# Seven seven-product squares in three FFN-down sweeps and five in the last, with transposes for the second and third norm at a later place

## The chip, the core and the metric

The kernel runs on one core of one Trainium2 chip. Measured is the device time of one execution in microseconds (us); the median over several executions is compared. On the core, TensorE (PE; its weight loads are listed apart as PEld), VectorE (DVE), ScalarE (ACT) and GpSimd (POOL) work side by side, and SyncE (SP) issues the DMA transfers that bring weights from the chip's memory. The engines wait for each other by semaphores.

## What is computed

One layer of a decoder trunk over 256 tokens with 2048 channels, in float32: a mixer (causal pooling and an RWKV-7 scan), a squared-ReLU MLP with 8192 hidden channels, a gated embedding and a last norm. The part that matters here:

```python
def rms_norm(x, g):
    xf = x.astype(jnp.float32)
    y = xf * lax.rsqrt(jnp.mean(xf * xf, axis=-1, keepdims=True) + NORM_EPS)
    return (y * g.astype(jnp.float32)).astype(x.dtype)
...
        x = x + mix @ w_out[i]

        h2 = rms_norm(x, mlp_norm[i])
        x = x + jnp.square(jax.nn.relu(h2 @ w_ffn_up[i])) @ w_ffn_down[i]

        gate = jax.nn.sigmoid(rms_norm(x, ple_norm[i]) @ w_ple_gate[i])
        x = x + gate * (p[i] @ w_ple_proj[i])
    return rms_norm(x, final_norm)
```

## The kernel before

**Numbers in two parts.** Float32 operands are split into a high and a low part that PE multiplies at its fast rate. A weight tile `raw` is loaded by SP; ACT writes its high part `wh`, DVE the rest `wl = raw - wh`. A product is three matmuls of 128x512: high by high (L1228), high by low (L1229), low by high (L1230).

**The stages** follow each other: the mixer, w_out (tiles `o`), FFN-up and FFN-down (`u`, `d`), the embedding product (`pp`), the gate (`gt`) and the end. x is kept as two tiles, x0 and x1, of 128 tokens by 2048 channels. The FFN is done in two halves of 4096 hidden channels. A half computes eight blocks `u` into activations `y`, and then makes two *sweeps* of FFN-down, one for each 1024 output columns: d00 and d01 for the first half, d10 and d11 for the second. The name is d, half, column pair.

**Squares.** A sweep has 16 *squares*, kp = 0 to 15. A square multiplies a 2 by 2 block of activations with a 2 by 2 block of weights (two loads of 512 KB, rx and ry). A *normal* square takes the eight products, 24 matmuls, and two split weight tiles (`a` and `b`, from `halves_of`, each 128x1024 on DVE). A *seven-product* square (Strassen's form in Winograd's variant; kp in `SEVEN`) takes seven, 21 matmuls, but needs sums of weight blocks: four DVE operations of 128x512 into `td` (L1268 to L1271), one more split `wad` (L172, L173), and three split tiles of 128x1024 (`b`, `c`, `d`). It also needs sums of activations (tile S), which `activation_sums` forms once in each FFN half, while `u` runs, for both sweeps. `SEVEN` holds six squares; the last sweep uses four of them (1, 3, 6, 11).

**Banks.** The products gather in eight banks of PSUM: four single ones (`d_b`, the output blocks of normal products) and two double ones (`d_w`: w16 and w57). The double ones are also those of `u` and of the transposes `h2t` and `h3t`. After the last seven-product square DVE adds the double banks to x (L1248, L1288, L1292), and they come free; after the last square, the four closing adds bring the single banks to x.

**Transposes for norms.** `transposed` gives a `part(norm, n)`: eight PE transposes of 512 columns of x into a double bank, then for each 128 columns ACT and DVE write the high part and the rest (L1140, L1141; rows named `h`). For the second norm, part n follows w_out's column block n; part 3 needs w_out's last residual adds (L1071). For the third norm, parts 0 and 1 are called as `between` in the last sweep, at the end of square 11, parts 2 and 3 after the sweep.

**Gate weights ahead of time.** `keep`, called by hooks ahead of the squares in positions 5, 8, 11 and 14 of the last sweep and later four times more, loads a gate weight tile `graw` (L1170), and splits it on ACT (L1174) and DVE (L1175) into `gk`. The tag `graw` has two buffers; both are also taken by the high and the low part of the `d` tile of a seven-product square. So a `graw` load can start when a seven-product square has ended, and the next `d` tile waits until `gk` has been split.

**What sets the order.** From w_out on, a scheduler orders each engine's instructions from the order of the program and priorities: weight splits and the adds at the end of a sweep have a higher one and come earlier than they are written. In the sweeps d00, d01 and d10 PE runs in the order of the program; in d11 pieces of neighbouring squares and the `h3t` transposes are interleaved.

Of the kernel before, what the change touches and what calls it, by code (L numbers as in the profile page):

```python
# [10 lines left out]
F32R = mybir.dt.float32r  # L11
# [29 lines left out]
def trunk(  # L41
# [1053 lines left out]
    def wide_bank(name):  # L1095
        return psw.tile([128, 2, 512], F32, tag="wide", name=name)

    def gemm_wide(src, acts, name, consume):

        for half in range(2):
            bank = wide_bank(f"{name}_w{half}")
            for kq in range(4):
                raw = load_raw(src[half, kq].rearrange("p a n -> p (a n)"), 1024, f"{name}{half}_{kq}")
                for a, (wh, wl) in enumerate(split_w(raw, f"{name}{half}_{kq}")):
                    for b in range(2):
                        k = kq * 4 + 2 * a + b
                        hl = acts(k)
                        cs = [slice(b * 256 + ct * 128, b * 256 + ct * 128 + 128) for ct in range(2)]  # L1110
                        for ct in range(2):
                            nc.tensor.matmul(  # L1112
                                bank[:, ct, :].rearrange("p (s t) -> p s t", s=2), wh[:, cs[ct]], hl,
                                start=k == 0, stop=False, skip_group_check=True,
                            )
                        for ct in range(2):
                            nc.tensor.matmul(  # L1117
                                bank[:, ct, 0:T], wl[:, cs[ct]], hl[:, 0, :], start=False, stop=k == 15, skip_group_check=True
                            )
            consume(half, bank)  # L1120
# [27 lines left out]
    deep.append("w_out")  # L1148
    for n in range(4):
        run(gemm_toks(w_out[n], mix, f"o{n}", lambda banks: residual(banks, n), (6, 7, 2, 3)))  # L1150
        h2_part("mlp_norm", n)


    s2 = const.tile([128, 2], F32, name="s2sq")
# [30 lines left out]

    SEVEN = (1, 3, 6, 8, 11, 13)
    s_slots = (0, 2, 5)

    def activation_sums(box, kp, r):

        i = SEVEN.index(kp)
        if i % 2 == 0:
            box[kp] = box[SEVEN[min(i + 1, len(SEVEN) - 1)]] = a8(s_slots[i // 2], f"S{kp}", F32R)
        st = box[kp][:, i % 2 * 1024 : i % 2 * 1024 + 1024]
        t_ = fp.tile([128, 1024], F32, tag="junk", bufs=1, name=f"s{kp}")
        s1, s2_, s3, s4 = (t_[:, j * 128 : (j + 1) * 128] for j in range(4))
        a11, a21, a12, a22 = (r[:, j * 128 : (j + 1) * 128] for j in range(4))
        nc.vector.tensor_tensor(s1, a21, a22, op=ALU.add)  # L1200
        nc.vector.tensor_tensor(s3, a11, a21, op=ALU.subtract)
        nc.vector.tensor_tensor(s2_, s1, a11, op=ALU.subtract)
        nc.vector.tensor_tensor(s4, a12, s2_, op=ALU.subtract)
        split_sb(st[:, 0:512], st[:, 512:1024], t_[:, 0:512])

    def down_sweep(hf, pair, ys, sboxes, hooks=(), between=None, seven=SEVEN):
# [40 lines left out]
        def add(tt, c, src):  # L1247
            nc.vector.scalar_tensor_tensor(xs(tt, c), src, s2[:, tt : tt + 1], xs(tt, c), op0=ALU.mult, op1=ALU.add)  # L1248

        for q, kp in enumerate((0, 2, 1, 4, 3, *range(5, 16)) if pair else range(16)):  # L1250
            if q in hooks:
                hooks[q]()
            y, j = ys[kp // 2], kp % 2 * 512
            a11, a21, a12, a22 = ((y[:, j + i * 128 : j + i * 128 + 128], y[:, 1024 + j + i * 128 : 1152 + j + i * 128]) for i in range(4))
            rx, ry = (load_raw(w_down[pair, hf * 32 + 2 * kp + i], 1024, f"{nm}_{kp}_{i}") for i in range(2))
            if kp in seven:
                i = SEVEN.index(kp)
                st = sboxes[kp][:, i % 2 * 1024 : i % 2 * 1024 + 1024]
                s1, s2_, s3, s4 = ((st[:, c * 128 : c * 128 + 128], st[:, 512 + c * 128 : 640 + c * 128]) for c in range(4))
                t_ = a8(1, f"t{nm}_{kp}")  # L1260
                t1, t3, t2, t4 = (t_[:, c * 512 : c * 512 + 512] for c in range(4))
                wa = fp.tile([128, 1024], F32R, tag="wa", name=f"wa{nm}_{kp}")
                w11 = wa[:, 0:512], wa[:, 512:1024]
                with tc.high_priority(20000):
                    split_sb(*w11, rx[:, 0:512])
                w21, w22 = halves_of(ry, f"{nm}_{kp}b")
                with tc.high_priority(20000):
                    nc.vector.tensor_tensor(t1, rx[:, 512:1024], rx[:, 0:512], op=ALU.subtract)  # L1268
                    nc.vector.tensor_tensor(t3, ry[:, 512:1024], rx[:, 512:1024], op=ALU.subtract)
                    nc.vector.tensor_tensor(t2, t3, rx[:, 0:512], op=ALU.add)  # L1270
                    nc.vector.tensor_tensor(t4, ry[:, 0:512], t2, op=ALU.subtract)  # L1271
                w1, w3 = halves_of(t_[:, 0:1024], f"{nm}_{kp}c")
                w2, w4 = halves_of(t_[:, 1024:2048], f"{nm}_{kp}d", True)
                for n, a_, w_ in (("1", a11, w11), ("2", a12, w21), ("3", s4, w22), ("5", s1, w1), ("7", s3, w3), ("6", s2_, w2), ("4", a22, w4)):
                    prod(n, a_, w_)
            else:
                w11, w12 = halves_of(rx, f"{nm}_{kp}a")
                for n, a_, w_ in (("2", a11, w11), ("4", a21, w11), ("3", a11, w12), ("x", a21, w12)):
                    prod(n, a_, w_)
                w21, w22 = halves_of(ry, f"{nm}_{kp}b")  # L1280
                for n, a_, w_ in (("2", a12, w21), ("4", a22, w21), ("3", a12, w22), ("x", a22, w22)):
                    prod(n, a_, w_)
            if kp == seven[-1]:
                u = fp.tile([128, 512], F32, tag="r", bufs=2, name=f"u{nm}")
                with tc.high_priority(20000):
                    add(0, 0, b1)
                    nc.scalar.activation(u, b1, AF.Copy)
                    nc.vector.tensor_tensor(u, b6, u, op=ALU.add)  # L1288
                    add(0, 1, b5)
                    add(1, 1, b5)  # L1290
                    add(0, 1, u)
                    nc.vector.tensor_tensor(u, b7, u, op=ALU.add)  # L1292
                add(1, 0, u)
                add(1, 1, u)
                if between is not None:
                    between()
        for n, tt, c in (("2", 0, 0), ("4", 1, 0), ("3", 0, 1), ("x", 1, 1)):
            with tc.high_priority(30000):
                add(tt, c, banks[n])
# [1 line left out]
    def ffn_half(hf):  # L1301
        sboxes = {}
        ys = []
        for i in range(8):
# [10 lines left out]
                if 2 * i + bi in SEVEN:  # L1315
                    activation_sums(sboxes, 2 * i + bi, r)

            gemm_wide(w_up[f], h2, f"u{f}", square)
            ys.append(y)
            if f == 1:  # L1320
                inv_ms()
# [6 lines left out]
        if hf == 0:  # L1328
            down_sweep(hf, 1, ys, sboxes)
        else:  # L1330
            down_sweep(hf, 1, ys, sboxes, {5: keep, 8: keep, 11: keep, 14: keep}, lambda: [h3_part("ple_norm", n) for n in range(2)], (1, 3, 6, 11))
            for n in range(2, 4):
                h3_part("ple_norm", n)

# [149 lines left out]
```

## Time and profile before

| what | us |
|---|---|
| median of three runs | 1184.19 |
| lowest, highest | 1183.07, 1185.29 |
| the profiled run | 1184.84 |
| span in its profile | 1183.1 |
| PE busy | 1166.3 |
| DVE busy | 857.5 |
| ACT busy | 704.5 |

The profile shows one execution. A row of a timeline has start, duration, engine, line and operation, the tiles written and read, and, in brackets, how long the engine was idle before it and what released it. Durations of matmuls overlap: their pace is the distance from one start to the next. A row with xN stands for N like instructions that follow each other. The chain of waits is followed back from the last instruction; a row of it is the time that a piece adds to the end. A table by stretches gives, for each stretch, its length and then the busy time and count of PE, PEld, DVE, ACT and POOL, the granted clock of PE, the busy share of the DMA engines and GB/s.

### The profile page before, as it was taken

What the parts mean: (1) busy time and instruction counts of PE and PEld (TensorE: products, weight loads), DVE (VectorE), ACT (ScalarE), POOL (GpSimd) and SP (SyncE); (2) the same over time, 40 slices, a digit from 0 to 9 for tenths busy, and PEclk for the clock granted to TensorE, in tenths of its full rate; (3) what the DMA queues carried; (4) which work ended last, traced back from release to release, by engine and by line L of the source; (5) the groups of instructions that cost most, each with busy time, mean ns of one, the idle gap of its engine ahead of it and who ended that gap; (6) DMA issues with size and microseconds to landing.
All of it is one profiled execution on the core that took longest, in us unless ns stands there. A gap on an engine that the chain in (4) does not pass through costs nothing.

```text
span 1183.1 us, 17263 instructions
## 1 busy us (share of the span) xinstructions
PE 1166.3 (99%) x6428; PEld 976.6 (83%) x6428; DVE 857.5 (72%) x1156; ACT 704.5 (60%) x1302; POOL 13.6 (1%) x73
## 2 busy tenths in 40 slices
PE   9999999999999999999999999999999999999997
PEld 8787777888887888888888888888888888878886
DVE  7686995964656666667888977666678779788543
ACT  7776848676545465555565654554556555668544
POOL 2100000000000000000000000000000000000000
PEclk9999999999999999999999999999999999999999
DMA  8464443354455555656556665655555556767611
GB/s 290 151 198 148 130 144 122 119 179 157 163 199 177 178 181 194 193 184 209 196 183 209 210 217 178 193 185 193 188 188 205 203 195 207 275 219 252 197 54 71
DMA packets 60756, 216.81 MB, mean 183 GB/s; under 512 B 6784, under 2 KB 7552, under 8 KB 60288
## 3 DMA queue, kind: packets, MB, share of 16 engines
q1 hardware_dynamic: 60240, 215.12, 54.5%
q8 instruction: 50, 0.82, 0.3%
q10 hardware_dynamic: 432, 0.60, 0.1%
q14 instruction: 34, 0.28, 0.1%
HBM read 213.59 MB, written 2.10 MB: 182 GB/s over the span
## 4 chain that ended last, share of the span: by engine, by line
PE 95%; ACT 2%; DVE 1%; DMA 1%; issue 0%; POOL 0%; SPq 0%; ACTq 0%; POOLq 0%
PE u_w L1112 20%; PE u_w L1117 10%; PE d_b L1229 8%; PE d_b L1230 8%; PE d_b L1228 8%; PE gt_b L238 2%; PE gt_b L242 2%; PE gt_b L241 2%; PE d_w L1229 2%; PE d_w L1230 2%; PE d_w L1228 2%; PE zk_b L241 1%; PE zk_b L242 1%; PE o_b L241 1%; PE o_b L242 1%; PE zv_b L238 1%
## 5 line engine op out<-in xcount | busy, mean ns | idle before, releaser
L1112 PE MATMUL u_w<-h,wh_u 128*128 128x512 f32 x1024 | 322.2, 396 | 0.0
L167 ACT ACTIVATE wh_u<-raw_u 128x512 fp32r<-128x512 f32 x256 | 147.6, 624 | 163.1 <-issue 96.1
L168 DVE TENSOR_TENSOR wl_u<-raw_u,wh_u 128x1024 fp32r<-128x1024 f32 x128 | 156.7, 1225 | 110.9 <-ACT wh_u L167 109.0
L1117 PEld LDWEIGHTS u_w<-h,wl_u 128*128 128x128 f32 x1024 | 192.5, 188 | 45.1
L1117 PE MATMUL u_w<-h,wl_u 128*128 128x256 f32 x1024 | 201.5, 278 | 0.0
L1112 PEld LDWEIGHTS u_w<-h,wh_u 128*128 128x128 f32 x1024 | 156.0, 189 | 0.1
L168 DVE TENSOR_TENSOR wl_gt<-raw_gt,wh_gt 128x1024 fp32r<-128x1024 f32 x24 | 29.4, 1224 | 23.2 <-ACT wh_gt L167 23.1
L167 ACT ACTIVATE wh_gt<-raw_gt 128x512 fp32r<-128x512 f32 x48 | 28.0, 639 | 23.1 <-PE gt_b L242 14.4
L241 PE MATMUL gt_b<-wh_gt,h 128*128 128x512 f32 x96 | 37.4, 389 | 0.0
L242 PE MATMUL gt_b<-wh_gt,h 128*128 128x512 f32 x96 | 37.4, 389 | 0.0
L168 DVE TENSOR_TENSOR wl_o<-raw_o,wh_o 128x1024 fp32r<-128x1024 f32 x16 | 19.6, 1223 | 12.9 <-ACT wh_o L167 9.9
L167 ACT ACTIVATE wh_o<-raw_o 128x512 fp32r<-128x512 f32 x32 | 18.4, 623 | 16.2 <-issue 8.4
L167 ACT ACTIVATE wh_zp<-raw_zp 128x512 fp32r<-128x512 f32 x32 | 18.6, 623 | 15.9 <-PE zp_b L242 5.7
L168 DVE TENSOR_TENSOR wl_zk<-raw_zk,wh_zk 128x1024 fp32r<-128x1024 f32 x16 | 19.5, 1222 | 9.4 <-ACT wh_zk L167 9.3
L241 PE MATMUL zv_b<-wh_zv,hTh 128*128 128x512 f32 x64 | 26.0, 407 | 0.0
L241 PE MATMUL zk_b<-wh_zk,hTh 128*128 128x512 f32 x64 | 25.8, 404 | 0.0
L241 PE MATMUL zp_b<-wh_zp,hTh 128*128 128x512 f32 x64 | 25.7, 402 | 0.0
L238 PE MATMUL gt_b<-wl_gt,h 128*128 128x512 f32 x96 | 25.7, 389 | 0.0
L242 PE MATMUL zk_b<-wh_zk,hTl 128*128 128x512 f32 x64 | 25.6, 401 | 0.0
L241 PE MATMUL zr_b<-wh_zr,hTh 128*128 128x512 f32 x64 | 25.5, 398 | 0.0
L168 DVE TENSOR_TENSOR wl_zv<-raw_zv,wh_zv 128x1024 fp32r<-128x1024 f32 x16 | 19.4, 1219 | 8.2 <-ACT wh_zv L167 7.3
L242 PE MATMUL zp_b<-wh_zp,hTl 128*128 128x512 f32 x64 | 25.0, 391 | 0.0
(809 smaller groups left out, 2941.4 us busy)
## 6 DMA issues: line engine op xcount, KB each, us to landing
raw_u<-in_w_ffn_up_dram SPq DMA_DIRECT2D x128, 512.0 KB, 3.5
raw_d<-in_w_ffn_down_dram SPq DMA_DIRECT2D x128, 512.0 KB, 4.3
raw_gt<-in_w_ple_gate_dram SPq DMA_DIRECT2D x24, 512.0 KB, 3.4
raw_zk<-in_w_in_dram SPq DMA_DIRECT2D x16, 512.0 KB, 3.6
raw_zr<-in_w_in_dram SPq DMA_DIRECT2D x16, 512.0 KB, 3.4
raw_zv<-in_w_in_dram SPq DMA_DIRECT2D x16, 512.0 KB, 3.4
raw_zp<-in_w_in_dram SPq DMA_DIRECT2D x16, 512.0 KB, 3.3
raw_o<-in_w_out_dram SPq DMA_DIRECT2D x16, 512.0 KB, 4.1
```

The lines of the kernel that those rows point to most:

```text
L167: nc.scalar.activation(wh[:, a * 512 : (a + 1) * 512], raw[:, a * 512 : (a + 1) * 512], AF.Copy)
L168: nc.vector.tensor_tensor(wl, raw, wh.bitcast(F32), op=ALU.subtract)
L238: nc.tensor.matmul(banks[tt], ah[:, ts_], halves[a][1], start=False, stop=last)
L241: nc.tensor.matmul(banks[tt], ah[:, ts_], halves[a][0], start=i + a == 0, stop=False)
L242: nc.tensor.matmul(banks[tt], al[:, ts_], halves[a][0], start=False, stop=False)
L1112: nc.tensor.matmul(bank[:, ct, :].rearrange("p (s t) -> p s t", s=2), wh[:, cs[ct]], hl, start=k == 0, stop=False, skip_group_check=True,)
L1117: nc.tensor.matmul(bank[:, ct, 0:T], wl[:, cs[ct]], hl[:, 0, :], start=False, stop=k == 15, skip_group_check=True)
L1228: nc.tensor.matmul(banks[n], ah, wh, start=first, stop=False)
L1229: nc.tensor.matmul(banks[n], ah, wl, start=False, stop=False)
L1230: nc.tensor.matmul(banks[n], al, wh, start=False, stop=last)
```

## The change

`SEVEN` gets a seventh square, and its squares are now all odd ones up to 13: in d00, d01 and d10 seven squares take seven products, in d11 five (1, 3, 7, 9, 11). The seventh set of activation sums lies in a tile of its own. Sweep d01 takes its squares in another order, so that normal and seven-product ones alternate; d00 and d10 alternate in their natural order; d11 keeps its order. Part 3 of the second norm's transposes is no longer called after w_out's last block but inside `u0`, ahead of the second of its four quarters. Parts 0 and 1 of the third norm's are called after square 12 instead of at the end of square 11.

```diff
-    def gemm_wide(src, acts, name, consume):
+    def gemm_wide(src, acts, name, consume, amid=None):
...
             for kq in range(4):
+                if amid and half == 0 and kq == 1:
+                    amid()
...
-        h2_part("mlp_norm", n)
+        if n < 3:
+            h2_part("mlp_norm", n)
...
-    SEVEN = (1, 3, 6, 8, 11, 13)
+    SEVEN = (1, 3, 5, 7, 9, 11, 13)
...
-            box[kp] = box[SEVEN[min(i + 1, len(SEVEN) - 1)]] = a8(s_slots[i // 2], f"S{kp}", F32R)
+            st = a8(s_slots[i // 2], f"S{kp}", F32R) if i < 6 else fp.tile([128, 1024], F32R, tag="S", name=f"S{kp}")
+            box[kp] = box[SEVEN[min(i + 1, len(SEVEN) - 1)]] = st
...
-        for q, kp in enumerate((0, 2, 1, 4, 3, *range(5, 16)) if pair else range(16)):
+        for q, kp in enumerate(((0, 2, 1, 4, 3, *range(5, 16)) if hf else (0, 2, 1, 4, 3, 6, 5, 8, 7, 10, 9, 12, 11, 14, 13, 15)) if pair else range(16)):
...
-                if between is not None:
-                    between()
+            if kp == seven[-1] + 1 and between is not None:
+                between()
...
-            gemm_wide(w_up[f], h2, f"u{f}", square)
+            gemm_wide(w_up[f], h2, f"u{f}", square, None if f else lambda: h2_part("mlp_norm", 3))
...
-            down_sweep(hf, 1, ys, sboxes, {5: keep, 8: keep, 11: keep, 14: keep}, lambda: [h3_part("ple_norm", n) for n in range(2)], (1, 3, 6, 11))
+            down_sweep(hf, 1, ys, sboxes, {5: keep, 8: keep, 11: keep, 14: keep}, lambda: [h3_part("ple_norm", n) for n in range(2)], (1, 3, 7, 9, 11))
```

In the code of the change the lines lie some further down: L1232 to L1234 are the three matmuls of a product, L1244 the DVE part of a split tile, L1252 an add to x, L1272 to L1275 the four `td`, L1173, L1177 and L1178 the rows of `keep`, L1136 the transposes, L1114 and L1119 the matmuls of `u`, L1143 the DVE part of `h`. The rows below show order alone.

PE at the end of w_out and the start of u0, before:

```order
L238 MATMUL o3_b1_3652<-wl_o3_3_3713,mp1_3213 128x512
L1134 MATMUL h2t_3731<-ident_85,x0_2724 128x128
L1112 MATMUL u0_w0_3750<-h2_3359,wh_u00_0_3753 128x512 x2
L1117 MATMUL u0_w0_3750<-h2_3359,wl_u00_0_3754 128x256
L1134 MATMUL h2t_3731<-ident_85,x1_2725 128x128
L1134 MATMUL h2t_3731<-ident_85,x0_2724 128x128
L1134 MATMUL h2t_3731<-ident_85,x1_2725 128x128
```

The same place with the change:

```order
L238 MATMUL o3_b1_3652<-wl_o3_3_3713,mp1_3213 128x512
L1114 MATMUL u0_w0_3733<-h2_3359,wh_u00_0_3736 128x512 x2
L1119 MATMUL u0_w0_3733<-h2_3359,wl_u00_0_3737 128x256 x2
...
L1136 MATMUL h2t_3757<-ident_85,x0_2724 128x128
L1136 MATMUL h2t_3757<-ident_85,x1_2725 128x128
L1136 MATMUL h2t_3757<-ident_85,x0_2724 128x128
L1136 MATMUL h2t_3757<-ident_85,x1_2725 128x128
L1114 MATMUL u0_w0_3733<-h2_3359,wh_u00_1_3776 128x512 x2
```

Before, the first transpose of the last part stands right behind w_out's last matmul; now the whole first quarter of u0 (the first two u0 rows, four times over) is ahead of it.

DVE in the last sweep, on the way to the sums of square 11, before (the number behind d11_ is the square, the letter its split tile; `td` and `wad` are the weight sums of a seven-product square, `gk` a kept gate tile):

```order
L1240 TENSOR_TENSOR wl_d11_9a_9496<-raw_d11_9_0_9491,wh_d11_9a_9495 128x1024
L1175 TENSOR_TENSOR gk2_9569<-graw2_9567,gk2_9569 128x1024
L1240 TENSOR_TENSOR wl_d11_9b_9513<-raw_d11_9_1_9493,wh_d11_9b_9512 128x1024
L1268 TENSOR_TENSOR td11_11_9577<-raw_d11_11_0_9573 128x512
L173 TENSOR_TENSOR wad11_11_9578<-raw_d11_11_0_9573,wad11_11_9578 128x512
L1269 TENSOR_TENSOR td11_11_9577<-raw_d11_11_1_9575,raw_d11_11_0_9573 128x512
...
L1240 TENSOR_TENSOR wl_d11_10b_9551<-raw_d11_10_1_9531,wh_d11_10b_9550 128x1024
L1240 TENSOR_TENSOR wl_d11_11d_9596<-td11_11_9577,wh_d11_11d_9595 128x1024
L1240 TENSOR_TENSOR wl_d11_11b_9582<-raw_d11_11_1_9575,wh_d11_11b_9581 128x1024
L1240 TENSOR_TENSOR wl_d11_11c_9591<-td11_11_9577,wh_d11_11c_9590 128x1024
```

With the change:

```order
L1244 TENSOR_TENSOR wl_d11_9c_9555<-td11_9_9541,wh_d11_9c_9554 128x1024
L1178 TENSOR_TENSOR gk1_9495<-graw1_9493,gk1_9495 128x1024
L1244 TENSOR_TENSOR wl_d11_9d_9560<-td11_9_9541,wh_d11_9d_9559 128x1024
L1244 TENSOR_TENSOR wl_d11_10a_9590<-raw_d11_10_0_9585,wh_d11_10a_9589 128x1024
...
L173 TENSOR_TENSOR wad11_11_9634<-raw_d11_11_0_9629,wad11_11_9634 128x512
L1244 TENSOR_TENSOR wl_d11_11b_9638<-raw_d11_11_1_9631,wh_d11_11b_9637 128x1024
...
L1244 TENSOR_TENSOR wl_d11_11c_9647<-td11_11_9633,wh_d11_11c_9646 128x1024
L1178 TENSOR_TENSOR gk2_9625<-graw2_9623,gk2_9625 128x1024
L1244 TENSOR_TENSOR wl_d11_12a_9692<-raw_d11_12_0_9687,wh_d11_12a_9691 128x1024
L1244 TENSOR_TENSOR wl_d11_11d_9652<-td11_11_9633,wh_d11_11d_9651 128x1024
```

Square 9 is a seven-product one now, gk1 stands ahead of its `d` tile, and gk2 ahead of that of square 11; before, gk2 came two squares earlier, and square 9 had no sums.

SP in the last sweep, before and with the change:

```order
L158 DMA raw_d11_8_0_9453<-in_w_ffn_down_dram 128x1024
L1170 DMA graw0_9317<-in_w_ple_gate_dram 128x1024
L158 DMA raw_d11_8_1_9455<-in_w_ffn_down_dram 128x1024
L158 DMA raw_d11_9_0_9491<-in_w_ffn_down_dram 128x1024
L158 DMA raw_d11_9_1_9493<-in_w_ffn_down_dram 128x1024
L1352 DMA fn_9961<-in_final_norm_dram 128x2048
```

```order
L158 DMA raw_d11_8_0_9499<-in_w_ffn_down_dram 128x1024
L1356 DMA fn_10017<-in_final_norm_dram 128x2048
L1173 DMA graw0_9363<-in_w_ple_gate_dram 128x1024
L158 DMA raw_d11_8_1_9501<-in_w_ffn_down_dram 128x1024
L158 DMA raw_d11_9_0_9537<-in_w_ffn_down_dram 128x1024
L158 DMA raw_d11_9_1_9539<-in_w_ffn_down_dram 128x1024
```

The load of the final norm's weights (`fn`, 1 MB) stands ahead of the first gate tile's now, not behind it.

## The prediction

> **What bounds the kernel now.** I read the page first, then the chain of waits, then the busy time by stretches of the four FFN-down sweeps.
>
> ```profile
> span 1183.1 us, 17263 instructions
> PE 1166.3 (99%) x6428; PEld 976.6 (83%) x6428; DVE 857.5 (72%) x1156; ACT 704.5 (60%) x1302; POOL 13.6 (1%) x73
> PE 95%; ACT 2%; DVE 1%; DMA 1%; issue 0%; POOL 0%; SPq 0%; ACTq 0%; POOLq 0%
> ...
> 650.25 0.91 PE d_b L1228 x4
> ...
> 638.00:723.00 85.00, 85.00 (x376) 70.33 (x375) 72.93 (x82) 48.37 (x84) 0.00 (x0) 1.00 0.61 203
> 981.00:1074.00 93.00, 91.99 (x414) 75.63 (x414) 78.03 (x90) 58.23 (x106) 0.00 (x0) 1.00 0.72 247
> ```
>
> PE is busy 99% of the span and makes 95% of the chain. In the stretches (span of the stretch, then PE, PEld, DVE, ACT) sweep d01 (638 to 723) has PE busy for all of its 85 us, with DVE at 72.9: matmuls set the time, and a matmul less is time less as long as DVE keeps up. The last sweep, d11 (981 to 1074), has 1 us of PE idle and DVE at 78 of 93: least room. The clock column is 1.00 in both. The chain gives the price of a 128x512 matmul: 0.91 / 4 = 0.2268 us (the 0.39 of a single row overlaps its neighbour).
>
> **The change, term by term.** The profiled run took 1184.84 us with a span of 1183.1; 1.74 lies around the span, and the run is 0.65 above the median of 1184.19. I sum on the span and carry the difference to the median.
>
> *Fewer matmuls.* One more seven-product square in each of four sweeps: 3 matmuls less each, 4 x 3 x 0.2268 = **-2.72 us**.
>
> *The wait at the second norm.* The chain at the end of w_out:
>
> ```profile
> 378.12 0.69 PE o_b L238 x3
> 378.81 0.02 issue
> 378.83 0.70 DVE x L1071
> 379.54 0.04 issue
> 379.58 0.33 PE h2t L1134
> ```
>
> PE stands from 378.81 to 379.58, 0.77 us, since the transposes of the last columns need the last residual add. Now the first quarter of u0 (8 matmuls of 0.23, 8 of 0.12: 2.8 us) stands ahead of them, against two adds of 0.70: covered. The transposed part is needed only by the last quarter of u0; it is ready about 0.8 us ahead. **-0.77**; without the cover 0.
>
> *The wait at the third norm.* The first four rows of h3:
>
> ```profile
> 1058.83 0.39 PE L1228 MATMUL d_b<-wh_d_13b,y 128*128 128x512 f32 x1
> 1060.22 0.98 PE L1134 MATMUL h3t<-ident,x 128*128 128x128 f32 x7 [1.01 <-DVE h L1141]
> ...
> 1058.55 1.23 DVE L1240 TENSOR_TENSOR wl_d_14a<-raw_d,wh_d_14a 128x1024 fp32r<-128x1024 f32 x1 [1.33 <-ACT wh_d_14a L1239]
> 1059.69 0.87 DVE L1141 SCALAR_TENSOR_TENSOR h<-h3t,par_sb,h 128x256 fp32r<-128x256 f32 x2
> ```
>
> The last matmul's pace ends at 1058.83 + 0.23 = 1059.06; the second transposes start at 1060.22, after DVE has read the bank behind wl_14a: 1.16 us. They now stand behind half of square 14: **-1.16** for the old wait; what the new place costs comes below. All gains: 2.72 + 0.77 + 1.16 = 4.65.
>
> *Three sweeps with alternating squares.* A seven square needs three halves (wl), four td, one wad on DVE, a normal one two halves. Sweep d01 already alternates in the middle, squares 5 to 8:
>
> ```profile
> 671.99 1.23 DVE L1240 TENSOR_TENSOR wl_d_6c<-td,wh_d_6c 128x1024 fp32r<-128x1024 f32 x1 [1.17 <-ACT wh_d_6c L1239]
> 675.53 0.39 PE L1229 MATMUL d_w<-wl_d_6c,S 128*128 128x512 f32 x1
> 682.19 1.23 DVE L1240 TENSOR_TENSOR wl_d_8c<-td,wh_d_8c 128x1024 fp32r<-128x1024 f32 x1 [1.09 <-ACT wh_d_8c L1239]
> 685.73 0.39 PE L1229 MATMUL d_w<-wl_d_8c,S 128*128 128x512 f32 x1
> ```
>
> From the end of wl_6c (673.22) to its use is 2.31 us, of wl_8c (683.42) again 2.31: over one alternating pair the lead doesn't shrink. By the paces below a pair costs DVE 5 x 1.13 + 5 x 0.61 = 8.7 us against 45 matmuls, 10.2. So 0 here. If the lead shrank all the same, the extra squares of these sweeps would give back their 9 x 0.2268 = 2.04.
>
> *Two more sets of activation sums*, one in each half:
>
> ```profile
> L173 DVE TENSOR_TENSOR S<-s,S 128x512 fp32r<-128x512 f32 x12 | 8.2, 684 | 0.0
> L1200 DVE TENSOR_TENSOR s<-r 128x128 f32<-128x128 f32 x12 | 3.5, 293 | 0.4
> L168 DVE TENSOR_TENSOR wl_u<-raw_u,wh_u 128x1024 fp32r<-128x1024 f32 x128 | 156.7, 1225 | 110.9 <-ACT wh_u L167 109.0
> ```
>
> A set is four 128x128 at 0.29 and one split at 0.68: 1.84 us of DVE, 3.7 for both. In FFN-up DVE stands idle 110.9 us ahead of its wl rows, which covers them: 0, and 3.7 if that cover were gone.
>
> *The last sweep.* Here the gate weights kept for the end (gk) share two buffers with the d halves of seven squares, so a load starts when a seven square ends and must be split before the next one's d half:
>
> ```profile
> 1011.87 0.39 PE L1230 MATMUL d_b<-wh_d_3d,y 128*128 128x512 f32 x1
> 1012.06 0.33 SPq L1170 DMA_DIRECT2D graw<-in_w_ple_gate_dram  x1
> 1017.46 1.15 ACT L1174 ACTIVATE gk<-graw 128x512 fp32r<-128x512 f32 x2 [1.23 <-DMA graw<-in_w_ple_gate_dram]
> 1018.64 1.23 DVE L1175 TENSOR_TENSOR gk<-graw,gk 128x1024 fp32r<-128x1024 f32 x1 [1.16 <-ACT gk L1174]
> 1019.90 1.23 DVE L1240 TENSOR_TENSOR wl_d_6d<-td,wh_d_6d 128x1024 fp32r<-128x1024 f32 x1
> 1021.18 0.51 PE L1229 MATMUL d_w<-wl_d_6d,S 128*128 128x512 f32 x1
> ...
> DMA to landing us min/median/max: 4.3/5.4/7.4
> ...
> fn<-in_final_norm_dram SPq DMA_DIRECT2D x1, 1024.0 KB, 9.1
> ```
>
> From issue (1012.06) to the end of wl_6d (1021.13) are 9.07 us; from the end of square 3 (1012.10) PE has 40 matmuls, 9.07, up to its use. It has no margin today, and the next pairs get the same or less. The paces of DVE and its adds:
>
> ```profile
> 1009.46 1.22 DVE L1240 TENSOR_TENSOR wl_d_5a<-raw_d,wh_d_5a 128x1024 fp32r<-128x1024 f32 x1
> 1010.59 0.68 DVE L173 TENSOR_TENSOR wad<-raw_d,wad 128x512 fp32r<-128x512 f32 x1
> 1011.20 1.22 DVE L1240 TENSOR_TENSOR wl_d_5b<-raw_d,wh_d_5b 128x1024 fp32r<-128x1024 f32 x1
> ...
> 1016.26 1.23 DVE L1240 TENSOR_TENSOR wl_d_6c<-td,wh_d_6c 128x1024 fp32r<-128x1024 f32 x1 [2.11 <-ACT wh_d_6c L1239]
> ...
> 1048.82 1.40 DVE L1248 SCALAR_TENSOR_TENSOR x<-d_w,s2sq,x 128x512 f32<-128x512 f32 x2
> ```
>
> That is 1.13 us for a 128x1024, 0.61 for a 128x512, 0.66 for an add; two h rows take 0.87 by the row above. Then, place by place:
>
> - Square 7. In DVE's new order wl_7c stands behind gk0. Its use is 58 matmuls (13.15 us) after the end of square 3; behind the landing come gk's 1.15 on ACT, two 1.2 on DVE and their handovers, 4.7, so the load must land within 8.45. A 5.4 does; but fn, 1 MB, now stands ahead of graw0 on SP, and a landing of 9.1 would cost 0.65. I take 0.
> - Square 9. Load 1 goes out at the end of square 7, 40 matmuls before wl_9d is used: the chain above again. 0 at 5.4, 2.0 at 7.4, a gain below nothing is excluded since PE can't be early. I take 0.
> - Square 11. From wl_9d to wl_11d DVE now has seven 1.13 and five 0.61, 11.05 with a handover, ahead of PE's 48 matmuls, 10.89; gk2 and ACT's rows between may add waits like those in brackets (2.11, 1.16). By load: 7.4 + 4.8 = 12.2 against 43 matmuls, 9.75, so up to 2.4. I take 1.2, half.
> - The h3 transposes in square 14. From wl_11d, DVE has seven 1.13 (12b to 15a with gk3 and gk4), three 0.61, six 0.66 and three h: 7.91 + 1.83 + 3.96 + 1.3 = 15.0, and 1.2 for a half of ACT at its end, 16.2. PE has 68 matmuls and 8 transposes, 15.42 + 0.9 = 16.3. 0 if all flows, 2.4 with the same lateness of a load again. I take 1.2.
> - The end. gk6 moves ahead of DVE's four closing adds: 0 if its load is in, 0.7 for what its 1.13 takes of them, 2 with a late load. I take 0.
>
> Sum of new stalls **+2.4** (0 to 8.8).
>
> On load 0 the Trainium skill ("DMA: Bandwidth & Descriptors", section "Queues, rings and completion order") says that each DMA engine serves one queue's ring in order, so that a transfer on the same queue as a large one lies behind it. By that rule graw0 would land as late as fn and the forecast would be 0.65 higher, 1182.5; in before, fn stood behind the gate load, and no row shows the reverse.
>
> Sum: 1183.1 - 4.65 + 2.4 = 1180.85 span, 1182.6 as a profiled run, and 1184.19 - 2.25 = **1181.9** as a median.
>
> **The rivals.**
>
> *Clean last sweep.* Loads land by their median, DVE runs without gaps: stalls of 0 to 1.2, 1179.5 to 1180.7, say 1180.1. For it speaks that each chain just fits; against it the gaps of 1 to 2 us in the DVE rows of this very place.
>
> *Slower: the gate loads are late.* The mechanism is the pair of shared buffers: a load can't start before a seven square ends, and with 7, 9, 11 in alternation there is one normal square, 40 matmuls, between. If each of them takes the 7.4 that one load took, the stalls are 2.0 + 2.4 + 2.4, and 2.0 at the end with gk6 ahead of the adds: 6.8 to 8.8, or 1186.3 to 1188.3. It decides from 4.65 of stalls (slower at all), 7.0 (slower beyond 0.2%). For it: this stretch moves 247 GB/s against 203 in d01. Against it: the median of the eight is 5.4, and a PE that stalls gives the next load its time.
>
> *The change doesn't do what it says.* The three earlier sweeps don't gain: DVE can't hold seven alternating pairs, and the 2.04 go into short waits at every seven square; with the last sweep as forecast 1181.9 + 2.0 = 1184.0. Against it stands the constant lead of 2.31.
>
> **How the numbers follow.** Forecast (stalls 1.2 to 4, 1180.7 to 1183.5): 0.53. Clean: 0.20. Late loads: 0.17. No gain in three sweeps: 0.10. The time is the forecast's, 1181.9. The range leaves out the lowest part of the clean case and most of the late one: 1179.6 to 1185.6; the forecast's own is 1180.7 to 1183.5. 0.2%, about what a measurement tells from no change, is 2.37 us: faster is below 1181.8, slower above 1186.6. Half of the forecast (0.26) and the clean case (0.20) make faster 0.46; the late loads beyond 7.0 (0.14) and some of the rest slower 0.15; same 0.39.
>
> **What would show it.** Right: PE's matmul count 12 lower; no wait between w_out and u0; no waits of PE in d00, d01, d10; in d11 waits of about 1 us ahead of wl_11d and of the transposes in square 14. The clean case shows none there; the late one shows graw landings above 7 and waits of 2 us at each d half, and at gk6 before the closing adds. The prediction is wrong if PE waits in the first three sweeps, or if the last one loses more than 4 us, or if u0's last quarter waits for the moved transposes.

## The result and the profile after

The changed kernel takes 1181.92 us (median of 21 runs, 1180.22 to 1183.86), the kernel before 1183.69 (21 runs, 1181.89 to 1185.65): a ratio of 0.9986, with a 95% interval of 0.9980 to 0.9992. The predicted time was 1181.9. The median of before that the prediction started from, 1184.19, came from three runs; from the larger set the gain is 1.77 us, not the 2.25 that was forecast.

The page of the changed kernel, first rows (span; busy time, share and count of each engine):

```profile
span 1181.2 us, 17297 instructions
PE 1163.6 (99%) x6416; PEld 973.0 (82%) x6416; DVE 876.1 (74%) x1190; ACT 713.2 (60%) x1316; POOL 13.6 (1%) x73
```

PE has 12 instructions less (6428 before), DVE 34 more. PE still sets the end: it makes 94% of the chain of waits. To see where the 1.9 us of span went, I cut the PE timeline at fixed matmuls, and read the same marks in each kernel. In the changed kernel (start, duration, engine, line, operation):

```profile
377.03 1.07 PE L238 MATMUL o_b<-wl_o,mp 128*128 128x512 f32 x4
...
557.33 0.40 PE L1232 MATMUL d_b<-wh_d_0a,y 128*128 128x512 f32 x1
...
721.99 0.61 PE L1114 MATMUL u_w<-h,wh_u 128*128 128x512 f32 x2
...
900.33 0.40 PE L1232 MATMUL d_b<-wh_d_0a,y 128*128 128x512 f32 x1
...
1069.83 0.39 PE L1234 MATMUL d_b<-wh_d_15b,y 128*128 128x512 f32 x1
...
1084.69 0.39 PE L241 MATMUL gt_b<-wh_gt,h 128*128 128x512 f32 x1
```

and in the kernel before:

```profile
377.95 1.07 PE L238 MATMUL o_b<-wl_o,mp 128*128 128x512 f32 x4
...
558.88 0.40 PE L1228 MATMUL d_b<-wh_d_0a,y 128*128 128x512 f32 x1
...
724.95 0.62 PE L1112 MATMUL u_w<-h,wh_u 128*128 128x512 f32 x2
...
903.28 0.40 PE L1228 MATMUL d_b<-wh_d_0a,y 128*128 128x512 f32 x1
...
1073.65 0.39 PE L1230 MATMUL d_b<-wh_d_15b,y 128*128 128x512 f32 x1
...
1086.61 0.39 PE L241 MATMUL gt_b<-wh_gt,h 128*128 128x512 f32 x1
```

The first mark is the end of w_out (the start of its last row plus four matmuls at 0.2268). Then follow the first matmul of d00, the first of the second FFN-up, the first of d10, the last of d11 and the first of the gate product. The table gives the distances, in us, for the two kernels and for every experiment below. "d00 and d01" goes from the first d00 matmul to the second FFN-up, "d10 and d11" from the first d10 matmul to the start of the last d11 matmul. "sum" is the whole stretch from the end of w_out to the start of the last matmul; it includes the second FFN-up (178.33 or 178.34 in all) and the gate product (87.55 to 87.60). The ratio is to runs of before on the same chip.

| kernel | w_out to d00 | d00 and d01 | d10 and d11 | d11 to gate | sum | median us | ratio to before, 95% |
|---|---|---|---|---|---|---|---|
| before | 180.02 | 166.07 | 170.37 | 12.96 | 795.30 | 1183.69 | |
| change | 179.39 | 164.66 | 169.50 | 14.86 | 794.30 | 1181.92 | 0.9986 (0.9980 to 0.9992) |
| change, again (fifth) | 179.37 | 164.60 | 169.54 | 14.27 | 793.67 | 1182.84 | 0.9990 (0.9981 to 0.9998) |
| 1 gk6 behind the adds | 179.39 | 165.01 | 169.24 | 13.00 | 792.52 | 1182.42 | 0.9986 (0.9977 to 0.9994) |
| 2 third norm as before | 179.39 | 164.62 | 168.66 | 12.95 | 791.50 | 1181.21 | 0.9980 (0.9970 to 0.9990) |
| 3 second norm as before | 180.04 | 164.62 | 170.02 | 14.24 | 794.81 | 1184.42 | 1.0002 (0.9994 to 1.0011) |
| 4 fewer gk in the sweep | 179.39 | 164.64 | 169.82 | 12.97 | 792.71 | 1183.05 | 0.9990 (0.9982 to 0.9999) |
| 6 as 4, third norm as before | 179.39 | 164.64 | 169.95 | 12.96 | 792.82 | 1182.30 | 0.9993 (0.9982 to 1.0003) |
| 7 six squares in d11 | 179.40 | 164.67 | 168.98 | 13.51 | 792.50 | 1182.56 | 0.9990 (0.9981 to 0.9999) |
| 8 d01 in old order | 179.39 | 164.65 | 170.85 | 13.95 | 794.73 | 1182.52 | 0.9992 (0.9983 to 1.0001) |
| 9 gk behind the sweep | 179.37 | 164.64 | 168.39 | 13.18 | 791.47 | 1179.89 | 0.9969 (0.9957 to 0.9981) |
| 10 as 9, six squares | 179.37 | 164.63 | 167.64 | 13.24 | 790.79 | 1179.17 | 0.9964 (0.9950 to 0.9978) |
| 11 moves alone | 179.39 | 165.97 | 169.75 | 13.92 | 794.92 | 1185.08 | 1.0009 (1.0000 to 1.0018) |
| 12 before, gk behind | 180.05 | 166.04 | 169.10 | 12.95 | 794.03 | 1183.57 | 0.9994 (0.9985 to 1.0003) |

Two things are read off it. The columns repeat within a few hundredths where PE never waits. (The 165.01 of the first experiment holds a stop of 0.36 at the start of d01, where DVE's closing add that frees the bank came late, after waits of ACT and DVE for the load of a down weight; no other profile has it.) The part ahead of w_out's end, in which these kernels are alike, does not: it ended between 377.19 and 379.93 us in these profiles, 378.86 in before and 377.94 in the change. So 0.92 of the 1.9 us between the two spans is no work of the change; from w_out on this profile has gained 1.00, its repetition 1.63.

Where the loss sits, in the last sweep of the changed kernel, PE and then DVE:

```profile
1044.00 0.39 PE L1232 MATMUL d_b<-wh_d_12a,y 128*128 128x512 f32 x1
1044.40 0.50 PE L1233 MATMUL d_b<-wl_d_12a,y 128*128 128x512 f32 x1
1045.53 0.50 PE L1233 MATMUL d_w<-wl_d_11d,S 128*128 128x512 f32 x1 [0.63 <-DVE wl_d_11d L1244]
```

```profile
1040.42 1.23 DVE L1244 TENSOR_TENSOR wl_d_11c<-td,wh_d_11c 128x1024 fp32r<-128x1024 f32 x1 [0.50 <-ACT wh_d_11c L1243]
1041.98 1.23 DVE L1178 TENSOR_TENSOR gk<-graw,gk 128x1024 fp32r<-128x1024 f32 x1 [0.34 <-ACT gk L1177]
1043.12 1.22 DVE L1244 TENSOR_TENSOR wl_d_12a<-raw_d,wh_d_12a 128x1024 fp32r<-128x1024 f32 x1
1044.26 1.22 DVE L1244 TENSOR_TENSOR wl_d_11d<-td,wh_d_11d 128x1024 fp32r<-128x1024 f32 x1
```

Matmuls that should start 0.23 apart start 0.40 and 1.13 apart: 0.17 + 0.90, since wl_11d is fourth in DVE's line behind gk2 and wl_12a. No load is late here, as ACT's row of gk2 has no wait in front:

```profile
1040.81 1.14 ACT L1177 ACTIVATE gk<-graw 128x512 fp32r<-128x512 f32 x2
```

And at the end of d11, PE, then ACT and DVE:

```profile
1069.83 0.39 PE L1234 MATMUL d_b<-wh_d_15b,y 128*128 128x512 f32 x1
1071.74 0.33 PE L1136 MATMUL h3t<-ident,x 128*128 128x128 f32 x1 [1.53 <-DVE x L1252]
...
1149.97 0.39 PE L1388 MATMUL gt3a<-gk,h 128*128 128x512 f32 x1
```

```profile
1066.56 0.63 ACT L1177 ACTIVATE gk<-graw 128x512 fp32r<-128x512 f32 x1 [1.91 <-DMA graw<-in_w_ple_gate_dram]
1067.10 1.14 ACT L167 ACTIVATE wh_pp<-raw_pp 128x512 fp32r<-128x512 f32 x2
```

```profile
1068.27 1.23 DVE L168 TENSOR_TENSOR wl_pp<-raw_pp,wh_pp 128x1024 fp32r<-128x1024 f32 x1 [2.20 <-ACT wh_pp L167]
1069.42 0.48 DVE L1143 SCALAR_TENSOR_TENSOR h<-h3t,par_sb,h 128x256 fp32r<-128x256 f32 x1
1069.81 1.22 DVE L1178 TENSOR_TENSOR gk<-graw,gk 128x1024 fp32r<-128x1024 f32 x1
1070.94 2.72 DVE L1252 SCALAR_TENSOR_TENSOR x<-d_b,s2sq,x 128x512 f32<-128x512 f32 x4
```

PE's pace ends at 1070.06 and the next transpose starts at 1071.74: 1.68 us. Read backwards, the rows name the chain: the transpose waits for x, whose adds stand on DVE behind gk6, h and wl_pp; wl_pp waited 2.20 for ACT; ACT stood 1.91 at gk6's high part, whose load had not landed. One late load of a kept tile, none of which PE uses before 1149.97, 83 us later, holds two engines. The load was late because it could not start before DVE had split gk4 and freed the buffer (DVE, then SP):

```profile
1059.48 1.22 DVE L1178 TENSOR_TENSOR gk<-graw,gk 128x1024 fp32r<-128x1024 f32 x1
```

```profile
1060.73 0.33 SPq L1173 DMA_DIRECT2D graw<-in_w_ple_gate_dram  x1
```

It landed 5.8 us after its issue, and ACT was ready for it at 1064.65, 3.9 us after the issue. Of the eight kept tiles only one landed faster than that (3.7).

### The profile page after: what moved, and what is told of

It is laid out like the page before. It is cut to its first block, busy times and chain, and to the rows that moved or that the text cites. A ratio compares the mean times of both kernels' runs of the same rounds, so it can differ in the third digit from the quotient of the medians.

```text
span 1181.2 us, 17297 instructions
## 1 busy us (share of the span) xinstructions
PE 1163.6 (99%) x6416; PEld 973.0 (82%) x6416; DVE 876.1 (74%) x1190; ACT 713.2 (60%) x1316; POOL 13.6 (1%) x73
## 4 chain that ended last, share of the span: by engine, by line
PE 94%; ACT 2%; DVE 2%; DMA 1%; issue 0%; SPq 0%; POOL 0%; DVEq 0%; ACTq 0%; POOLq 0%
PE u_w L1114 20%; PE u_w L1119 10%; PE d_b L1233 7%; PE d_b L1232 7%; PE d_b L1234 7%; PE d_w L1233 2%; PE d_w L1234 2%; PE d_w L1232 2%; PE gt_b L242 2%; PE gt_b L241 2%; PE gt_b L238 2%; PE zk_b L241 1%; PE zk_b L242 1%; PE o_b L238 1%; PE o_b L241 1%; PE o_b L242 1%
## 5 line engine op out<-in xcount | busy, mean ns | idle before, releaser
L1114 PE MATMUL u_w<-h,wh_u 128*128 128x512 f32 x1024 | 321.7, 395 | 0.0
L1119 PEld LDWEIGHTS u_w<-h,wl_u 128*128 128x128 f32 x1024 | 192.4, 188 | 45.4
L1119 PE MATMUL u_w<-h,wl_u 128*128 128x256 f32 x1024 | 201.4, 278 | 0.0
L1114 PEld LDWEIGHTS u_w<-h,wh_u 128*128 128x128 f32 x1024 | 156.0, 189 | 0.2
L167 ACT ACTIVATE wh_zk<-raw_zk 128x512 fp32r<-128x512 f32 x32 | 18.4, 623 | 10.9 <-PE zv_b L242 4.0
```

Source lines behind the costliest of these rows:

```text
L167: nc.scalar.activation(wh[:, a * 512 : (a + 1) * 512], raw[:, a * 512 : (a + 1) * 512], AF.Copy)
L1114: nc.tensor.matmul(bank[:, ct, :].rearrange("p (s t) -> p s t", s=2), wh[:, cs[ct]], hl, start=k == 0, stop=False, skip_group_check=True,)
L1119: nc.tensor.matmul(bank[:, ct, 0:T], wl[:, cs[ct]], hl[:, 0, :], start=False, stop=k == 15, skip_group_check=True)
```

## The experiments

The line gated into `keep` in several of them makes the load of a gate tile wait for the last closing add:

```diff
     def keep():
...
+        if kp == 6:
+            nc.vector.tensor_scalar_mul(raw[:, 0:1], xr[1][:, 2047:2048], s2[:, 0:1])
         nc.sync.dma_start(raw, w_gate[3, kp].rearrange("p a n -> p (a n)"))
```

**1. gk6 behind the closing adds**: the diff above and nothing else.

> The changed kernel with one addition: the load of the seventh kept gate tile waits for the closing add of x1, so that gk6 stands behind the four closing adds on DVE and its high part no longer holds up ACT. In the changed kernel the first gate matmul comes 14.9 us after the last d11 matmul (12.8 before), with a PE wait of 1.68. Theory A (gk6's place in the queues of ACT and DVE causes the wait): 12.8 to 13.3, the rest as in the changed kernel, about 1.8 us below it. Theory B (the faster sweep leaves DVE and ACT behind whatever the order): at least 1 us of wait stays.

The first gate matmul came 13.00 us after d11, not 14.86. Now wh_pp starts more than two us earlier against the last matmuls, and the adds wait for PE, not PE for the adds (ACT, then DVE of this kernel):

```profile
1065.16 1.15 ACT L167 ACTIVATE wh_pp<-raw_pp 128x512 fp32r<-128x512 f32 x2 [0.20 <-PE d_b L1236]
```

```profile
1066.34 1.23 DVE L168 TENSOR_TENSOR wl_pp<-raw_pp,wh_pp 128x1024 fp32r<-128x1024 f32 x1
1067.48 0.48 DVE L1143 SCALAR_TENSOR_TENSOR h<-h3t,par_sb,h 128x256 fp32r<-128x256 f32 x1
1068.51 2.80 DVE L1254 SCALAR_TENSOR_TENSOR x<-d_b,s2sq,x 128x512 f32<-128x512 f32 x4 [0.54 <-PE d_b L1236]
```

A holds for the end of the sweep: the wait comes from gk6 in that place, not from a lack of engine time. The median shows less than the rows (1182.42, against 1182.84 of the change's repetition); the intervals are wide enough for both.

**2. The third norm's parts at their old place** (`if kp == seven[-1]`, at the end of square 11).

> The changed kernel with the third norm's parts 0 and 1 called at the end of square 11 as before. The scheduler then also places gk6 behind the closing adds. Theory A: the wait at the second h3 transposes comes back (1.2 us, against 0.3 in the changed kernel) and the 2.0 us of the end go: about 1.1 us below the changed kernel. Theory B: the end keeps its wait, and the kernel is about 0.9 us above the changed one. The wait at wl_11d stays at about 1.2 by both.

The end was cured as by A (12.95). But no wait of 1.2 came back at the h3 transposes: d10 and d11 took 168.66, less than with the move. The only wait of d11 here is the one at wl_11d, 0.85:

```profile
1044.14 0.50 PE L1233 MATMUL d_w<-wl_d_11d,S 128*128 128x512 f32 x1 [0.64 <-DVE wl_d_11d L1244]
```

In this profile the old place has no such wait. So with five squares the move of the third norm's transposes shows no gain; what it did was to put gk6 ahead of the adds, where the scheduler has it behind them here.

**3. The second norm's part 3 at its old place.**

> The changed kernel with the second norm's part 3 called after the last w_out block as before. My term: 0.77 us between w_out's last matmul and the next PE work comes back, nothing else moves. Rival: the moved transposes gain nothing, because the time comes back in the later quarters of u0 (under 0.2 us).

The wait is back, and from w_out to d00 the kernel takes 180.04 again, 0.65 more than the change (PE; then a wait in d11):

```profile
380.65 0.33 PE L1136 MATMUL h2t<-ident,x 128*128 128x128 f32 x1 [0.56 <-DVE x L1071]
...
1024.83 0.50 PE L1232 MATMUL d_w<-wl_d_7c,S 128*128 128x512 f32 x1 [0.47 <-DVE wl_d_7c L1243]
```

The term is real, a little smaller than the 0.77 expected, and nothing is paid back later in u0. The second row was not expected in this kernel, and is the place of square 7: here the first gate tile took 8.9 us to land, behind fn's 8.1. With the two late starts around that row the place costs 0.74.

**4. Fewer kept tiles in the sweep** (three hooks in d11, at 5, 8 and 14, and five in the gate stage; `if kp > 4`, so that tiles 5 to 7 load behind the closing adds).

> The changed kernel with the kept gate tiles moved: three hooks in the last sweep (positions 5, 8, 14), five in the gate stage, and tiles 5 to 7 loaded only after the closing add of x1. On DVE no gk stands between the d tiles of squares 9 and 11, nor ahead of the closing adds. Theory A: the wait at wl_11d (1.2) and that of the end (2.0) both go, about 3 us below the changed kernel. Theory B: the waits move to the gate stage or stay at the end, under 1 us gained.

Both waits went, as A says, but a new one of 1.49 came at the h3 transposes of square 13, so that of about 3 us 1.6 remained in the sum (PE, and ACT at gk2 before it):

```profile
1058.48 0.66 PE L1136 MATMUL h3t<-ident,x 128*128 128x128 f32 x4 [1.49 <-DVE h L1143]
```

```profile
1052.66 1.15 ACT L1179 ACTIVATE gk<-graw 128x512 fp32r<-128x512 f32 x2 [2.80 <-DMA graw<-in_w_ple_gate_dram]
```

**5. The changed kernel again.**

> The changed kernel again, beside the others of this set: how much of its first profile repeats. From the last w_out matmul on, PE took 795.3 us in before and 794.3 in the changed kernel. Theory A, that gk6's place makes the wait of the end: the first gate matmul again 14 to 15 us after the last d11 matmul, the wait at wl_11d 1.2. If the wait of the end was a chance of one execution: about 13.

14.27 us from d11 to the gate, with a wait of 0.95 at the first transpose by its row, and again 0.63 at wl_11d. The wait of the end repeats, and its size follows the load. Four profiles have this code at the end: the change, this one, the third and the eighth experiment. ACT's wait at gk6 is 1.91, 1.34, 1.34 and 0.99 in them, and the way from d11 to the gate is 1.90, 1.31, 1.28 and 0.99 longer than the 12.96 of before. So the loss follows the late load nearly one to one, and no more is left that gk6's own 1.13 on DVE would have to explain. The stop at wl_11d is the same in all four, 0.9, with no wait of ACT at gk2: there it is the place alone.

**6. As 4, with the third norm's parts at the old place.**

> The changed kernel with the third norm's parts at the old place (end of square 11), three keep hooks in the last sweep (positions 5, 8, 14) and five in the gate stage, tiles 5 to 7 loaded after the closing add of x1: no gk between the d tiles of squares 9 and 11. Theory A, that the wait at wl_11d comes from gk2 and wl_12a ahead of it on DVE: the wait of 1.2 goes. If the place of the h3 transposes is then as tight as in before, 1.2 comes back there and the sum is that of the second experiment (791.5 us from the last w_out matmul); if not, 790.3.

No wait at wl_11d, but 1.51 at the h3 transposes: 792.82, worse than either forecast. ACT of this kernel names the cause:

```profile
1053.62 1.15 ACT L1179 ACTIVATE gk<-graw 128x512 fp32r<-128x512 f32 x2 [2.31 <-DMA graw<-in_w_ple_gate_dram]
1054.68 0.46 ACT L1142 ACTIVATE h<-h3t,par_sb 128x256 fp32r<-128x256 f32 x1
1055.03 0.62 ACT L1179 ACTIVATE gk<-graw 128x512 fp32r<-128x512 f32 x1
1055.55 1.14 ACT L1245 ACTIVATE wh_d_14a<-raw_d 128x512 fp32r<-128x512 f32 x2
```

A kept tile again, now gk2: ACT stands 2.31 at it, and h, wh_14a and then DVE's h rows come late. It is the picture of the end, at another place. So the theory widened: not only at the place ahead of the adds, any kept tile that ACT or DVE reaches before its load has landed holds what is behind it.

**7. Six seven-product squares in the last sweep**, in alternating order, with the kept tiles as they are.

> The changed kernel with six seven-product squares in the last sweep, in alternating order (0 2 1 4 3 6 5 8 7 10 9 12 11 13 14 15), and the third norm's parts at the old place. Three matmuls less than the second experiment: 790.8 us from the last w_out matmul if DVE keeps up as it does in the other sweeps. Theory of the tight sweep (gate tiles and sums share DVE and the two buffers): new waits at d tiles of more than the 0.7 won.

792.50: 1.0 above the second experiment where 0.7 less was expected, with waits at wl_7d, wl_11d and, behind the sweep, an h3 transpose. The theory of the tight sweep holds for this kernel, as long as the kept tiles stand in it (see the tenth).

**8. Sweep d01 in its old order.**

> The changed kernel with sweep d01 in its old order (0 2 1 4 3 5 6 7 8 ...) and the new seven-product squares: 3 and 5 then stand side by side, the rest alternates. My step that the alternating order costs nothing on PE: one pair of neighbours gives a wait of at most 1 us in d01, and the order of the change saves that. From first d00 to the first matmul of the second FFN half the changed kernel took 164.66; expected here 164.7 to 165.7.

d00 and d01 took 164.65, as with the new order (164.66): two neighbouring seven-product squares cost nothing, and the reordering of d01 is worth nothing here. The last sweep, the same code as in the change, took 1.35 more this time. Square 9, a place that the prediction named and put at 0, costs 1.40 here:

```profile
1033.81 0.50 PE L1233 MATMUL d_w<-wl_d_9d,S 128*128 128x512 f32 x1 [1.13 <-DVE wl_d_9d L1244]
```

and on ACT:

```profile
1030.08 1.15 ACT L1177 ACTIVATE gk<-graw 128x512 fp32r<-128x512 f32 x2 [2.40 <-DMA graw<-in_w_ple_gate_dram]
```

ACT stood 2.40 at gk1.

**9. Kept tiles behind the sweep**: two hooks in d11, six in the gate stage (`if kp > 1`), the third norm's parts at the old place, and

```diff
-                    nc.scalar.activation(h[:, j, :], src, AF.Copy, scale=col(norm, j))
...
+                    with tc.high_priority(25000):
+                        nc.scalar.activation(h[:, j, :], src, AF.Copy, scale=col(norm, j))
...
```

> The changed kernel with the third norm's parts at the old place and its h rows at the priority of the splits, and with six of the eight kept gate tiles loaded after the closing add of x1 (two in the last sweep). Nothing but splits, sums and h rows is left on DVE from square 9 on. Theory A, that every wait of the last sweep comes from gk rows or splits standing ahead of what PE needs next: no wait at wl_11d, none at the h3 transposes, none at the end: 795.30 - 0.65 - 2.72 - 1.16 = 790.8 us from the last w_out matmul on, 3.5 below the changed kernel. Theory B, that the sweep has too little DVE and ACT time for five squares: a wait of 1 us or more comes back somewhere in d11, or the gate stage takes more than its 87.55.

791.47, 2.8 below the change's first profile and 2.2 below its second, where 790.8 was expected. The waits at wl_11d and the end are gone, and the gate stage keeps its 87.55. What is left: 0.51 at wl_9d, which still waits for gk1, 0.14 at a transpose, and 0.2 at the end. Three things were changed at once here, and the sum is that of the second experiment (791.50), which moved the transposes back and no more. So by the sums the kept tiles' new place shows no gain over that one; one profile of each can't tell whether gk1's late load hid it.

**10. All eight kept tiles behind the sweep, six squares in d11.**

> As the ninth, with all eight kept gate tiles behind the closing adds and six seven-product squares in the last sweep in alternating order. Theory A: three matmuls less, 790.1 us from the last w_out matmul, no wait in d11. Theory B: waits at d tiles in d11 of more than 0.7, or a gate stage longer than 87.55 because eight tiles of 512 KB more are loaded in it.

790.79, three matmuls (0.68) below the ninth, with one wait left in d11. It is about as long as the two waits of the ninth together, so that the match is partly chance. Against the seventh experiment, which has the same squares but the kept tiles in the sweep and the h rows at the old priority, it is 1.71. PE, then ACT:

```profile
1052.57 0.66 PE L1136 MATMUL h3t<-ident,x 128*128 128x128 f32 x4 [0.50 <-DVE ud L1295]
```

```profile
1050.67 0.63 ACT L172 ACTIVATE ph<-raw_pT 128x512 fp32r<-128x512 f32 x1 [1.49 <-DMA raw_pT<-in_pT_dram]
1051.21 0.58 ACT L1294 ACTIVATE ud<-d_w 128x512 f32<-128x512 f32 x1
```

This wait is no kept tile's, but of the same kind: ACT stands 1.49 at the input of the embedding product (raw_pT), whose load has not landed, and `ud`, which frees the bank, comes late.

It is the fastest kernel of this study, 1179.17 us: a ratio of 0.9964 (0.9950 to 0.9978) to before, below the change's interval. The gate stage, with all eight loads in it, takes 0.03 more.

**11. The two moves alone**, with the old squares.

> The changed kernel with the old squares (1, 3, 6, 8, 11, 13 and 1, 3, 6, 11 in the last sweep, old order in d01); the two moves of the transposes alone. By my terms the second norm's move gives 0.65 and the third norm's 1.16: 793.5 us from the last w_out matmul. Rival: the second h3 transposes wait at their new place too, or the end does, and 794.6 or more is left.

794.92: the rival. The second norm gives its 0.63. In d10 and d11 0.62 are won, as the second h3 transposes still wait 0.59 at their new place. At the end 0.96 are lost, where gk6 stands ahead of the adds here too. The median of 1185.08 lies above before's although the sum lies 0.38 below. In its profile the part ahead of w_out's end took 379.59, the second longest; whether it was as long in the other nine runs is not shown.

**12. The kernel before, with its kept tiles behind the sweep** (`if True`, no hooks in d11), and no other edit. The scheduler puts the second h3 transposes behind 13b's second matmul and 14a's second, where they stood behind 13b's fourth.

> The kernel before with one thing changed: all eight kept gate tiles are loaded after the closing add of x1, none in the last sweep. Theory A, that the old wait of 1.16 at the third norm's transposes was made by ACT standing at a kept tile whose load had not landed: the wait goes without any move of the transposes, dn1 (first d10 to last d11 matmul) 169.2 instead of 170.37, and from the last w_out matmul 794.1 instead of 795.30. Theory B, that the wait is the price of the transposes' old place: it stays at 1 us or more.

169.10 and 794.03, and no wait of PE in d11 at all. The first four of these transposes come two matmuls earlier here and still don't wait, so it isn't their place that removed the wait. The old wait of 1.16 was a kept tile's as well, and this is its row in the kernel before:

```profile
1056.84 0.63 ACT L1174 ACTIVATE gk<-graw 128x512 fp32r<-128x512 f32 x1 [1.04 <-DMA graw<-in_w_ple_gate_dram]
1057.38 1.14 ACT L1239 ACTIVATE wh_d_14a<-raw_d 128x512 fp32r<-128x512 f32 x2
```

wl_14a waited 1.33 for that wh_14a, and the h rows stood behind it. The median (1183.57) can't tell 1.3 us from nothing.

## Why the prediction was right, and where its sum was not

The time lies inside the range and the forecast's own range; that it agrees to 0.02 us is luck. The median that it started from was 0.50 above that of the larger set, and the forecast gain was 0.48 too large, which cancels; and single steps are off by up to 1.9 us, in both directions.

- *Twelve matmuls, -2.72*: right. d00 and d01 are 1.41 shorter for six matmuls (1.36 by pace). (0.91 / 4 is 0.2275, not 0.2268; the starts of the rows lie 0.2268 apart, and the term is the same to 0.01.)
- *Second norm, -0.77*: right in mechanism, 0.63 to 0.65 in size (third experiment).
- *Alternating squares and the sums at 0*: right. In both profiles of the change PE has no wait in d00, d01 and d10, and the second FFN-up takes 178.34 against 178.33. The old order of d01 does as well (eighth experiment).
- *Old wait of the third norm, -1.16*: gone, but the move was not needed for it. I took the wait for a price of the place; the sixth and twelfth experiments show a kept tile's load in front of wh_14a.
- *Square 7 at 0*: right in the change; 0.74 in the third experiment, a little above the 0.65 allowed. (The bound of all stalls, 8.8, leaves this 0.65 out.)
- *Square 9 at 0*: 0.30 in the change (0.19 ahead of the wl_9d row, 0.11 behind it), 0.42 in its repetition and 1.40 in the eighth experiment. The chain without margin was read rightly, and 0 was its best case.
- *Square 11 at 1.2*: 0.17 + 0.90 + 0.11 behind the row, 1.18. The size is right; of the two reasons given it was gk2's place in the line, not a late load.
- *Transposes in square 14 at 1.2*: 0.27. Gk3 and gk4 were in time, so the half of the late case that was taken was too much.
- *The end at 0*: 1.90 in the change (14.86 - 12.96), 1.31 in its repetition. This is the step that failed. The bound of 2 with a late load stood in the text, and 0 was taken with no reason beside it. The rows of before spoke against it: ACT waits 0.69 to 1.62 us for the load at six of the eight kept tiles there. Even the median landing would not have done: 4.7 us after the issue is 0.8 later than ACT came to it.

The new stalls add up to 0.30 + 1.18 + 0.27 + 1.90 = 3.65 where 2.4 was forecast (3.1 in the repetition, with 1.31 at the end), and -2.72 - 0.63 - 1.16 + 3.65 = -0.86 is the measured -1.00 within 0.14. So the slower rival was half there: a late load held PE at the end. But its condition did not hold, since behind the first tile none took more than 5.8 us to land in the change; the load was late because it was issued late. The sum of stalls stayed below 4.65, and the gain was not used up.

Whether fn ahead of the first gate tile matters was left between two answers. The landings in the changed kernel, gate tiles first, then fn:

```profile
DMA to landing us min/median/max: 3.7/4.7/7.9
```

```profile
DMA to landing us min/median/max: 7.0/7.0/7.0
```

The 7.9 is the first gate tile's, issued 0.46 us behind fn: it lands 1.4 us after fn, and takes 7.9 where the median is 4.7. That agrees with the Trainium skill ("DMA: Bandwidth & Descriptors", section "Queues, rings and completion order"), by which each DMA engine consumes descriptors in the order of the ring; the section promises no order in which writes finish. The time of 7.9 is below the 8.45 at which it would have cost PE time, and the 8.9 of the third experiment is above it.

What stays open is how the waits of d11 are spread over executions; each kernel was read in one profile, the change in two. Why the stages ahead of w_out vary by up to 2.7 us is shown in part, in the last section.

## What to carry to other kernels

A prefetch that is split by an engine with work for the critical path is not free because the engine has idle time: its row stands in the engine's line, and a load that is not there when the engine comes to it holds all that is behind it (1.91 us of ACT became 1.90 us of the end here). Let such a load start where nothing urgent stands behind its split, or where its buffer comes free early enough for the landing. Here the place behind the closing adds did that, at no cost in the gate stage: 1.8 us for gk6 alone in the change (first experiment), 1.3 for all eight in the kernel before (twelfth). With the transposes moved back as in the second experiment, nothing more was gained by it with five squares (ninth). When gains are a few tenths of a per cent, compare the distance between fixed instructions, not whole executions.

## What the runs showed beyond that

The profile puts a wait of PE or DVE down to its last releaser. For the waits at h, x and wl_14a that were traced here, the origin lay two or three steps back, in an ACT row with "<-DMA graw" in its bracket. The stop at wl_11d is an exception, with no late load behind it.

A 512 KB load behind a 1 MB one on the same queue took 6.3 to 8.9 us to land. In the kernels that issue the first gate tile behind fn and keep four hooks in the sweep, the median of the gate tiles is 4.6 to 5.1.

The first 378 us of one and the same code took between 377.19 and 379.93 us, and a part of that is the clock. Between 38 and 44 us the mean granted clock of PE is 0.72 in the first row (third experiment) and 1.00 in the second (second experiment):

```profile
38.00:44.00 6.00, 5.89 (x22) 4.77 (x23) 4.33 (x14) 3.66 (x7) 2.55 (x9) 0.72 0.32 109
```

```profile
38.00:44.00 6.00, 6.00 (x30) 5.04 (x29) 5.28 (x15) 4.00 (x7) 2.32 (x8) 1.00 0.31 102
```

In the slow stretch the matmuls start 0.43 apart, not 0.23:

```profile
39.40 0.63 PE L241 MATMUL zk_b<-wh_zk,hTh 128*128 128x512 f32 x1
39.83 0.63 PE L242 MATMUL zk_b<-wh_zk,hTl 128*128 128x512 f32 x1
```

Seven of the fourteen profiles have such a stretch there, of four to eight matmuls, 0.8 to 1.6 us in all; before, the change and its repetition have none. Behind it, at the 241st matmul, the profiles stand between 47.5 and 49.7 us; from there to the end of w_out they differ by 0.9 at most. The mean clock of the whole span, 0.996 to 0.998 in all of them, doesn't show it. What starts the slow stretch in one execution and not in another is not shown.
